# The delta-rule chain of a hybrid layer: full-height residual, cleared coupling block, loads as buffers come free, and a replanned schedule

## Chip, cores and metric

The kernel runs on one core of a Trainium2 chip. The metric is the device time of one launch in microseconds (us); the time of the kernel before is the median of three runs.

## What is computed

One layer of a streaming encoder over 2048 positions of width 1024, all in fp32. The part around the change is the gated DeltaNet branch, 8 heads of width 128 in chunks of 64 positions:

```python
A = jnp.where(strict, jnp.einsum('bhnik,bhnjk->bhnij', k_beta, k) * L, 0.0)
T = lax.linalg.triangular_solve(A + eye, eye, left_side=True, lower=True, unit_diagonal=True)
u = jnp.einsum('bhnij,bhnjv->bhniv', T, v * beta[..., None])
w = jnp.einsum('bhnij,bhnjk->bhnik', T, k_beta * jnp.exp(decay)[..., None])
def step(state, inp):
    v_new = u_c - jnp.einsum('bhck,bhkv->bhcv', w_c, state)
    o_c = q_c @ state + qk_c @ v_new
    state = state * a_c + jnp.einsum('bhck,bhcv->bhkv', k_c, v_new)
```

Around it stand an RMSNorm and one combined input projection ahead, a gMLP branch (gelu, LayerNorm, a masked 128x128 spatial mixing, a SiLU gate) beside it, and an output projection, a gated per-layer embedding and a last RMSNorm behind it.

## The kernel before

**Work.** The positions are taken in two passes of 1024. In each pass the projection (tile `pj`) goes through the heads; a head has three units of weights (k and q; v and the gMLP's u; the two gates z). Every projection product is three matmuls of 512 columns on rounded high and low parts (`mm3`: `hi*hi`, `hi*lo`, `lo*hi`). Behind the heads of both passes come the output projection (`pso`), the gate (`pg`) and the embedding.

**The branch of one head** runs as a row of tasks, two blocks of 512 positions each (b = 0, 1), four units of 128 positions (two chunks) per block:
- `decay` makes the mask tile `L` (POOL cuts it, line 184).
- `front` (line 729) transposes k into PSUM tile `pk`, squares it, makes `pkq` (k against k and q), and from it `AT`, the system's matrix times its mask (DVE), whose block [64:128, 0:64] couples the second chunk to the first (ACT). The diagonal blocks go to DRAM (`atd`).
- `root` and `side` make 1/norm of k (`iv`, a power on POOL) and the scaled v (`vn`); `side` transposes q and v (`pq`, `pvt`).
- `inverse` (line 833) solves the 64x64 triangular systems of the head on POOL: 63 columns, a multiply (`xtmp`) and a subtraction (`xs`) for each. The systems come back from DRAM four columns at a time in 16 loads `ain` with four buffers, issued on SP's queue; the solution goes to DRAM (`td`) and from there into the diagonal blocks of `AT` (here called `M`).
- `join` (line 883) multiplies the inverse of one chunk by the coupling block (`pgt`) and puts the product into the upper right block of `M`.
- `chain` (line 896) is the recurrence, eight units in a row for each head, each of four links that wait for one another: a matmul into `pc`, then an evacuation on DVE or ACT, then the next matmul. S to r: `pc<-S,kq`, then DVE makes the lower half of r in a tile `r0` whose upper half is zero. r0 to r: `pc<-r0,AT`, then ACT writes the lower half of `r` from PSUM and DVE its upper half. r to w: `pc<-r,AT`, then ACT writes the lower half of `w`, DVE the upper. w to S: `pc<-w,kd`, then DVE makes the new state S.
- `finish` (line 974) normalises the output (`sso`, a power on POOL), transposes it (`po_t`) and multiplies by the gate (`zb`).

The tiles `pk`, `pq`, `pvt`, `pgt` and `po_t` share two PSUM banks (tag "tr"), so each of their users waits until the one before last has been read.

**What sets the order.** The order of the instructions on every engine is planned by hand, in Python. `Flow` keeps a planned clock `fl.t` for PE, advanced by each matmul (lines 121 to 130), and one for DVE, ACT and POOL, advanced by a cost for each operation (lines 135 to 185). A task yields the planned time at which it wants to go on; until then the projection's matmuls are issued. So a chain link's planned duration says how many `pj` matmuls stand on PE between two matmuls of the chain. A delay `LAZY` says how long after its inputs a power or a mask is put on POOL. The costs set the order only; at run time every engine goes in its order and waits for semaphores.

Of the kernel before, what the change touches and what calls it, by code (L numbers as in the profile page):

```python
# [101 lines left out]

LAZY = 4000.0
CAPS = {"pj": 2, "tr": 2, "m": 2, "kq": 5, "pre": 2, "acc": 3, "uz": 3, "ot": 2, "gn": 2, "R": 2, "raw": 4, "w": 5}
# [3 lines left out]
def trunk(tc, a, out):  # L108
# [9 lines left out]
    def width(ap):  # L118
        return int(np.prod(ap.shape[1:]))
# [59 lines left out]
    def gtt(o, x, y, op, after=None):  # L179
        nc.gpsimd.tensor_tensor(o, x, y, op)  # L180
        return fl.op("pool", 375 + 1.95 * width(o), after)

# [4 lines left out]
    with ExitStack() as outer:  # L187
# [541 lines left out]
        def front(p, h, b, st):  # L729
# [9 lines left out]
            iv = gt("iv", "iv", [P, 4], 4)  # L739
            fb = gt("fb", "fb", [P, 4], 4)  # L740
            qe = gt("qe", "qe", [P, 4], 6)
            kd = gt("kd", "kd", [P, 4, P], 4)
# [13 lines left out]
            tt(bn, bn, beta[:, cs], ALU.mult)  # L756
            tt(fb, bn, ex[:, 3, cs], ALU.mult)
            fl.spawn(root(b, st, iv), f + LAZY - fl.t, 1)
            AT = gt("AT", "AT", [P, 4, P], 4)
            QK = gt("QK", "QK", [P, 4, P], 4)  # L760
            for u2 in range(2):
                while len(st["C"][b]) < 2:
                    yield fl.t + 300
                yield from fl.take("R", 2)
                hi = gt("R", "kqhi", [P, 2, 2, P], 2, F32R)
                lo = gt("R", "kqlo", [P, 2, 2, P], 2, F32R)
                yield from split_to(hi, lo, kq[:, u2 * 2:u2 * 2 + 2])
                yield fl.clk["dve"] + 120
                yield from fl.take("m")
                pkq = bank("m", "pkq", [P, 2, 2, P])  # L770
                for j in range(2):
                    for x, y in ((hi, hi), (hi, lo), (lo, hi)):
                        f = mm(pkq[:, j], x[:, j, 0], y[:, j], x is y, x is lo)
                fl.give("R")
                fl.give("R")
                while len(Ls) <= st["i"] + b:
                    yield fl.t + 300
                L = Ls[st["i"] + b]
                yield f
                for j in range(2):  # L780
                    u = u2 * 2 + j
                    yield from fl.room("dve")
                    f = stt(AT[:, u], pkq[:, j, 0], bn[:, u:u + 1], L[:, u], ALU.mult, ALU.mult)
                    act(AT[64:128, u, 0:64], pkq[64:128, j, 0, 0:64], AF.Copy, after=f,
                        scale=ex[64:128, 3, h * 8 + b * 4 + u:h * 8 + b * 4 + u + 1])
                yield from fl.room("dve")
                f = tt(QK[:, u2 * 2:u2 * 2 + 2], pkq[:, :, 1], L[:, u2 * 2:u2 * 2 + 2], ALU.mult)
                fl.give("m")
# [9 lines left out]
            fl.spawn(side(b, st, kq, vn, iv, ss, qe), 0, 2)  # L798
            st["B"].append((kq, kd, vn, AT, QK, bn, fb, qe))
            if b == 1:  # L800
# [32 lines left out]
        def inverse(p, h, st):  # L833
# [3 lines left out]
            def load(jc):  # L837
                ains[jc] = gt("ain", "ain", [P, 4, 64], 4)
                dma(ains[jc].rearrange("p j i -> p (j i)"),
                    asys[None, :, jc * 256:(jc + 1) * 256].to_broadcast([8, 16, 256]))  # L840
            while 2 * len(solved) < st["i"]:
                yield fl.t + 300
            xs = gt("xs", "xs", [P, 8, 64], 2)
            dma(xs, a["xinit"])
            load(0)
            while 2 * len(inverted) < st["i"]:
                yield fl.t + 300
            for jc in range(1, 4):
                load(jc)
            tmp = gt("xtmp", "xtmp", [P, 160], 1)  # L850
            yield fl.t + (1000 if h else 4500)
            for j in range(63):
# [8 lines left out]
                if jj == 3:  # L861
                    yield f
                    if jc < 12:
                        load(jc + 4)
                    elif jc == 12:
                        solved.append(1)
            yield f
            td = dp.tile([64, 2, 4, 2, 64], F32, tag="td", bufs=2, name="td")
            dma(td.rearrange("(k c) b u d i -> (c b u d) k i", c=8), xs)
            inverted.append(1)  # L870
            yield fl.t + 2600
# [11 lines left out]
        def join(b, st):  # L883
# [8 lines left out]
            fl.give("tr")  # L892
            yield f
            st["G"].append(b)

        def chain(p, h, st):
# [6 lines left out]
            for b in range(2):  # L903
                kq, kd, vn, M, QK, bn, fb, qe = st["B"][b]
                yield from fl.take("ot")
                ot = gt("ot", "ot", [P, 4, P], 2)
                sso = gt("sso", "sso", [P, 4], 2)
                for u in range(4):
# [7 lines left out]
                    if first:  # L916
                        f = vcopy(r0[lo], vn[lo, u])
                    else:
                        yield mm(pc[:, 0], kq[:, u, 0, :], Sp, True, True)
                        f = stt(r0[lo], pc[lo, 0], ne[lo, cu], vn[lo, u], ALU.mult, ALU.add)  # L920
                    yield f
                    f = mm(pc[:, 1], M[:, u], r0, True, True)
                    while outs[-1:] == [0]:
                        yield fl.t + 100
                    po = bank("o", "po", [P, 2, P])
                    if not first:
                        mm(po[:, 0], kq[:, u, 1, :], Sp, True, True)
                    yield f
                    f = act(r[lo], pc[lo, 1], AF.Copy, scale=-1.0)
                    if first:  # L930
                        f2 = vcopy(r[up], vn[up, u])
                    else:
                        f2 = stt(r[up], pc[up, 0], ne[up, cu], vn[up, u], ALU.mult, ALU.add)
                    yield max(f, f2)
                    while len(st["G"]) <= b:
                        yield fl.t + 100
                    f = mm(pc[:, 2], M[:, u], r, True, True)
                    yield f
                    f = act(w[lo], pc[lo, 1], AF.Copy, scale=bn[lo, uu])
                    yield max(f, ts(w[up], pc[up, 2], bn[up, uu], None, ALU.mult))  # L940
                    more = not (last and p == NPASS - 1)
# [5 lines left out]
                    if more:  # L947
                        yield f
                        Sn = gt("S", "S", [P, P], 2)
                        if first:  # L950
                            f = vcopy(Sn, pc[:, 3])
                        else:
                            f = stt(Sn, Sp, ex[:, 2, cu], pc[:, 3], ALU.mult, ALU.add)
                        Sp = Sn
                        yield f
                        if last:
                            dma(ssc[h], Sn)
# [364 lines left out]

        done, chained, fronts, solved, inverted, SC, mixed, stored, vdone, prepped, Ls = [[] for _ in range(11)]
        xready = [0, 0]
# [27 lines left out]
        X0 = x_tiles()  # L1352
        r0 = gt("r0", "r0", [P, P], 1)

        def setup():
            nc.vector.memset(r0, 0.0)
            fl.op("dve", 200)
            act(nega, nega, AF.Exp)
            ts(nega, nega, -1.0, None, ALU.mult)
            yield  # L1360
# [72 lines left out]
```

## Time and profile before

| | us |
|---|---|
| median of three runs | 2354.44 (2354.35 to 2355.75) |
| profiled execution, its own time | 2356.51 |
| its span | 2354.8 |
| PE matmul busy | 2284.6 (97%) |
| PE weight loads busy | 1873.9 (80%) |
| DVE busy | 1353.5 (57%) |
| ACT busy | 1115.8 (47%) |
| POOL busy | 1127.1 (48%) |
| mean granted TensorE clock | 0.993 |
| DMA moved | 254.59 MB, 108 GB/s |

The span is the profiler's, from first to last instruction; the execution's own time is what the device reported for the same run, so 1.7 us lie around the span. Busy times of PE overlap (a matmul's record begins before the one ahead has ended), so a PE that is 97% busy is not 3% from its floor. A bracket behind a row of the timeline is the idle time of the engine just before it and what ended it. Waits of an engine that nobody waits for cost nothing.

### The profile page before, as it was taken

How to read it: one execution, taken by the hardware profiler on the slowest of the kernel's cores; microseconds unless marked ns; L12 is line 12 of the kernel's file. 1: busy time of each engine (PE TensorE's matmuls, PEld its weight loads, DVE VectorE, ACT ScalarE, POOL GpSimd, SP SyncE). 2: the span in 40 equal slices, each digit the busy share in tenths (PEclk: the TensorE clock that was granted, in tenths of full speed). 3: DMA queues.
4: the chain of work that ended last, by engine and by line, in shares of the span. 5: the costliest groups of instructions: out<-in, count | busy, mean ns of one | idle time of the engine just before them, and what ended most of it. 6: DMA issues, size and time to landing. Idle time of an engine off the chain costs nothing.

```text
span 2354.8 us, 35453 instructions
## 1 busy us (share of the span) xinstructions
PE 2284.6 (97%) x11888; PEld 1873.9 (80%) x11888; DVE 1353.5 (57%) x2948; ACT 1115.8 (47%) x2665; POOL 1127.1 (48%) x2246
## 2 busy tenths in 40 slices
PE   8999999999999989999999999999999999999998
PEld 8978777777777779978787787777777878878886
DVE  5465566575675664456567567576564343246665
ACT  5554465464554643446446455464443232234443
POOL 1118677676676672147677667677680000001111
PEclk9999999999999999999999999999999999999999
DMA  5633332323323343223232332322453466452221
GB/s 188 222 105 97 99 87 75 96 68 100 97 78 98 90 131 100 82 77 89 81 96 70 98 100 70 106 76 81 124 177 109 144 202 195 139 186 65 81 81 63
DMA packets 269431, 254.59 MB, mean 108 GB/s; under 512 B 67904, under 2 KB 200512, under 8 KB 269248
## 3 DMA queue, kind: packets, MB, share of 16 engines
q1 hardware_dynamic: 269248, 252.32, 35.1%
q8 instruction: 93, 1.52, 0.3%
q14 instruction: 90, 0.74, 0.1%
HBM read 196.68 MB, written 55.57 MB: 107 GB/s over the span
## 4 chain that ended last, share of the span: by engine, by line
PE 76%; DVE 10%; ACT 7%; DMA 3%; issue 3%; SPq 1%; POOL 0%; ACTq 0%; DVEq 0%; POOLq 0%
PE pj L122 32%; PE pso L122 13%; PE pv L122 7%; PE pg L122 7%; PE pc L122 6%; DVE acc L153 2%; PE pe L122 2%; ACT junk L136 2%; PE po L122 2%; PE pm L122 1%; PE pgt L122 1%; PE pkq L122 1%; DVE wlo L149 1%; DVE AT L153 1%; ACT AT L136 1%
## 5 line engine op out<-in xcount | busy, mean ns | idle before, releaser
L180 POOL TENSOR_TENSOR xtmp<-ain,xs 128x132 f32<-128x132 f32 (+47 forms) x1008 | 464.6, 461 | 235.4 <-DMA ain<-atd 166.9
L180 POOL TENSOR_TENSOR xs<-xs,xtmp 128x132 f32<-128x132 f32 (+47 forms) x1008 | 480.1, 476 | 79.0
L176 POOL TENSOR_TENSOR rstd<-rstd,nhalf 128x1 f32<-128x1 f32 x64 | 46.0, 724 | 578.6 <-DVE rstd L160 297.6
L122 PE MATMUL pj<-xrhi,wlo 128*128 128x512 f32 x768 | 313.8, 409 | 0.0
L122 PE MATMUL pj<-xrhi,whi 128*128 128x512 f32 x768 | 309.3, 403 | 4.0 <-ACT u L136 4.0
L122 PE MATMUL pj<-xhi,wlo 128*128 128x512 f32 x768 | 310.2, 404 | 0.0
L122 PE MATMUL pj<-xhi,whi 128*128 128x512 f32 x768 | 310.1, 404 | 0.0
L122 PE MATMUL pj<-xlo,whi 128*128 128x512 f32 x768 | 310.0, 404 | 0.0
L122 PE MATMUL pj<-xrlo,whi 128*128 128x512 f32 x768 | 309.5, 403 | 0.0
L153 DVE SCALAR_TENSOR_TENSOR acc<-pre,cw,acc 128x512 f32<-128x512 f32 x288 | 226.9, 788 | 30.5 <-ACT acc L136 26.5
L149 DVE TENSOR_TENSOR wlo<-raw,whi 128x512 fp32r<-128x512 f32 x224 | 166.1, 746 | 83.4 <-ACT whi L136 82.1
L122 PE MATMUL pso<-wolo,yhi 128*128 128x512 f32 x512 | 204.7, 400 | 1.1 <-DVE wolo L149 1.1
L122 PE MATMUL pso<-wohi,ylo 128*128 128x512 f32 x512 | 204.8, 400 | 0.0
L122 PE MATMUL pso<-wohi,yhi 128*128 128x512 f32 x512 | 202.5, 395 | 1.2 <-ACT zb L136 1.2
L136 ACT ACTIVATE yhi<-yraw 128x512 fp32r<-128x512 f32 x128 | 80.2, 629 | 214.1 <-PE pso L122 202.4
L149 DVE TENSOR_TENSOR ylo<-yraw,yhi 128x512 fp32r<-128x512 f32 x128 | 89.5, 701 | 148.8 <-ACT yhi L136 146.5
L122 PEld LDWEIGHTS pj<-xrhi,whi 128*128 128x128 f32 x768 | 145.7, 190 | 30.0 <-ACT u L136 4.4
L122 PEld LDWEIGHTS pj<-xrlo,whi 128*128 128x128 f32 x768 | 145.3, 189 | 27.5
L122 PEld LDWEIGHTS pj<-xhi,wlo 128*128 128x128 f32 x768 | 145.1, 189 | 26.2
L122 PEld LDWEIGHTS pj<-xlo,whi 128*128 128x128 f32 x768 | 145.1, 189 | 25.7
L122 PEld LDWEIGHTS pj<-xhi,whi 128*128 128x128 f32 x768 | 145.2, 189 | 25.5
L122 PEld LDWEIGHTS pj<-xrhi,wlo 128*128 128x128 f32 x768 | 145.6, 190 | 25.0
(195 smaller groups left out, 4972.5 us busy)
## 6 DMA issues: line engine op xcount, KB each, us to landing
raw<-in_wu SPq DMA_DIRECT2D x224, 256.0 KB
ain<-atd SPq DMA_DIRECT2D x256, 128.0 KB
yraw<-ysc SPq DMA_DIRECT2D x128, 256.0 KB
vsc<-gv SPq DMA_DIRECT2D x64, 128.0 KB
gn<-vsc SPq DMA_DIRECT2D x32, 256.0 KB
ysc<-gn SPq DMA_DIRECT2D x32, 256.0 KB
ysc<-zb SPq DMA_DIRECT2D x32, 256.0 KB
wo<-in_wo SPq DMA_DIRECT2D x32, 256.0 KB
```

The costliest lines, as they stand in the source:

```text
L122: nc.tensor.matmul(o, lhsT, rhs, start=start, stop=stop)
L136: nc.scalar.activation(o, i, func, **kw)
L149: nc.vector.tensor_tensor(o, x, y, op)
L153: nc.vector.scalar_tensor_tensor(o, x, sc, y, op0, op1)
L176: nc.gpsimd.tensor_tensor(o, x, y, ALU.pow)
L180: nc.gpsimd.tensor_tensor(o, x, y, op)
```

## The change

1. Chain: `r` is made by one DVE operation over all 128 rows. The coupling block of `M` is cleared behind `join`, so that the first product needs no zero half; `r0` is gone. ACT then overwrites the lower half of `r`, and the lower half of `w` is made on ACT from `r` in SBUF with a new factor `nb` = -`bn`, no longer from PSUM beside DVE's half.
2. Planner: each link's planned end gets `SPARE` (120 ns) more; the links' ACT and DVE halves are no longer planned as parallel; the planned cost of POOL's solve operations goes down; `LAZY` from 4000 to 7000 ns.
3. `front`: the coupling blocks of two units are made by one DVE operation in place of two on ACT.
4. `inverse`: each of the first four loads of a system is issued as soon as one buffer is free in the plan, all behind the solution's `td` of the head before.

```diff
-LAZY = 4000.0
+LAZY = 7000.0
+SPARE = 120.0
...
     def gtt(o, x, y, op, after=None):
-        return fl.op("pool", 375 + 1.95 * width(o), after)
+        return fl.op("pool", 345 + 1.7 * width(o), after)
...
+            ts(nb, bn, -1.0, None, ALU.mult)
...
-                    f = stt(AT[:, u], pkq[:, j, 0], bn[:, u:u + 1], L[:, u], ALU.mult, ALU.mult)
-                    act(AT[64:128, u, 0:64], pkq[64:128, j, 0, 0:64], AF.Copy, after=f,
-                        scale=ex[64:128, 3, h * 8 + b * 4 + u:h * 8 + b * 4 + u + 1])
+                    stt(AT[:, u], pkq[:, j, 0], bn[:, u:u + 1], L[:, u], ALU.mult, ALU.mult)
+                us = slice(u2 * 2, u2 * 2 + 2)
+                c = h * 8 + b * 4 + u2 * 2
+                tt(AT[64:128, us, 0:64], pkq[64:128, :, 0, 0:64],
+                   ex[64:128, 3, c:c + 2, None].to_broadcast([64, 2, 64]), ALU.mult)
...
-            while 2 * len(solved) < st["i"]:
-                yield fl.t + 300
             xs = gt("xs", "xs", [P, 8, 64], 2)
-            dma(xs, a["xinit"])
-            load(0)
-            while 2 * len(inverted) < st["i"]:
-                yield fl.t + 300
-            for jc in range(1, 4):
+            for jc in range(4):
+                while len(solved) <= 2 * st["i"] - 4 + jc:
+                    yield fl.t + 300
+                if jc == 0:
+                    dma(xs, a["xinit"])
                 load(jc)
+                since = fl.t if jc == 0 else since
             tmp = gt("xtmp", "xtmp", [P, 160], 1)
-            yield fl.t + (1000 if h else 4500)
+            yield max(fl.t, since + 4500)
...
-                    elif jc == 12:
+                    else:
                         solved.append(1)
             yield f
+            solved.append(1)
...
-            yield f
+            nc.vector.memset(M[64:128, :, 0:64], 0.0)
+            yield fl.op("dve", 250) + SPARE
...
-                        f = stt(r0[lo], pc[lo, 0], ne[lo, cu], vn[lo, u], ALU.mult, ALU.add)
-                    yield f
-                    f = mm(pc[:, 1], M[:, u], r0, True, True)
+                        f = stt(r, pc[:, 0], ne[:, cu], vn[:, u], ALU.mult, ALU.add)
+                    yield f + SPARE
+                    while len(st["G"]) <= b:
+                        yield fl.t + 100
+                    f = mm(pc[:, 1], M[:, u], r, True, True)
...
-                    yield f
-                    f = act(r[lo], pc[lo, 1], AF.Copy, scale=-1.0)
-                    if first:
-                        f2 = vcopy(r[up], vn[up, u])
-                    else:
-                        f2 = stt(r[up], pc[up, 0], ne[up, cu], vn[up, u], ALU.mult, ALU.add)
-                    yield max(f, f2)
-                    while len(st["G"]) <= b:
-                        yield fl.t + 100
+                    yield f + SPARE
+                    yield act(r[lo], pc[lo, 1], AF.Copy, scale=-1.0) + SPARE
                     f = mm(pc[:, 2], M[:, u], r, True, True)
-                    yield f
-                    f = act(w[lo], pc[lo, 1], AF.Copy, scale=bn[lo, uu])
-                    yield max(f, ts(w[up], pc[up, 2], bn[up, uu], None, ALU.mult))
+                    act(w[lo], r[lo], AF.Copy, scale=nb[lo, uu])
+                    yield f + SPARE
+                    yield ts(w[up], pc[up, 2], bn[up, uu], None, ALU.mult) + SPARE
```

The order changes with the plan. **PE, the third unit of the fourth head's chain in the first pass**, before (`r_220` is the tile `r0`, `r` the full one):

```order
L122 MATMUL pc<-r_220,AT 128x128
L122 MATMUL po<-S,kq 128x128
L122 MATMUL pj<-xlo,whi 128x512
L122 MATMUL pj<-xhi,wlo 128x512
L122 MATMUL pc<-r,AT 128x128
L122 MATMUL pj<-xhi,whi 128x512
L122 MATMUL pj<-xlo,whi 128x512
L122 MATMUL pj<-xhi,wlo 128x512
L122 MATMUL pc<-w,kd 128x128
```

and the same unit now:

```order
L123 MATMUL pc<-r,AT 128x128
L123 MATMUL po<-S,kq 128x128
L123 MATMUL pj<-xhi,wlo 128x512
L123 MATMUL pj<-xhi,whi 128x512
L123 MATMUL pj<-xlo,whi 128x512
L123 MATMUL pc<-r,AT 128x128
L123 MATMUL pj<-xhi,wlo 128x512
L123 MATMUL pj<-xhi,whi 128x512
L123 MATMUL pj<-xlo,whi 128x512
L123 MATMUL pj<-xhi,wlo 128x512
L123 MATMUL pj<-xhi,whi 128x512
L123 MATMUL pc<-w,kd 128x128
```

Between the first and the second product with `AT` three projection matmuls stand where two stood, and ahead of the product with `w` five where three stood.

**SP's queue where the fourth head's solve ends**, before:

```order
L839 DMA ain<-atd 128x1x256 x2
L796 DMA atd<-AT 64x4x64 x2
L844 DMA xs<-in_xinit 128x512
L839 DMA ain<-atd 128x1x256
L650 DMA ws<-in_ws 128x128
L653 DMA bs<-in_bs 128x128
L253 DMA raw<-in_wu 128x512 x4
L660 DMA gn<-vsc_73 128x4x128 x2
L869 DMA td<-xs 128x8x64
L839 DMA ain<-atd 128x1x256 x3
L875 DMA AT<-td 64x4x64 x4
```

and now:

```order
L874 DMA td<-xs 128x8x64
L801 DMA atd<-AT 64x4x64 x2
L879 DMA AT<-td 64x4x64 x4
L851 DMA xs<-in_xinit 128x512
L844 DMA ain<-atd 128x1x256 x4
L651 DMA ws<-in_ws 128x128
L654 DMA bs<-in_bs 128x128
L254 DMA raw<-in_wu 128x512 x4
L661 DMA gn<-vsc_73 128x4x128 x2
```

The next head's `xs` and first `ain` stood ahead of `td`, and three further `ain` between `td` and `AT<-td`; now `td`, the second half of `atd` and `AT<-td` stand ahead of all of them, and the loads of weights behind.

**PE, the transposes of the sixth head's front** (k in `pk`, q in `pq`) beside those of a finished output block (`po_t`), before:

```order
L122 MATMUL pj<-xhi,whi 128x512
L128 MATMUL po_t<-ident,ot 128x128 x4
L128 MATMUL pk<-ident,kq 128x128 x4
L122 MATMUL pj<-xlo,whi 128x512
L128 MATMUL pq<-ident,kq 128x128 x4
L122 MATMUL pj<-xhi,wlo 128x512
```

and now:

```order
L129 MATMUL pq<-ident,kq 128x128 x4
L129 MATMUL pk<-ident,kq 128x128 x4
L123 MATMUL pj<-xhi,wlo 128x512
L123 MATMUL pj<-xhi,whi 128x512
L123 MATMUL pj<-xlo,whi 128x512
L123 MATMUL pj<-xhi,wlo 128x512
L123 MATMUL pj<-xhi,whi 128x512
L123 MATMUL pj<-xlo,whi 128x512
L123 MATMUL pj<-xhi,wlo 128x512
L123 MATMUL pj<-xhi,whi 128x512
L123 MATMUL pj<-xlo,whi 128x512
L129 MATMUL po_t<-ident,ot 128x128 x4
```

`po_t` no longer stands directly ahead of the front's transposes but nine projection matmuls behind them.

## Rows read from the trace of the kernel before

**Rows 1.** PE by line: instructions | busy us, mean ns | idle before, releasers.

```profile
L122 PE MATMUL pc<-r,AT 128*128 128x128 f32 x512 | 109.0, 295 | 6.9 <-DVE r L153 0.9
L122 PE MATMUL pc<-w,kd 128*128 128x128 f32 x240 | 54.6, 309 | 7.2 <-DVE w L158 2.6
L122 PE MATMUL pc<-S,kq 128*128 128x128 f32 x240 | 51.7, 297 | 3.9 <-DVE S L153 2.9 <-DMA S<-ssc 0.7
```

**Rows 2.** Tile pc: waits of its weight loads on PE, us and times.

```profile
  PEld pc L122: 104.4, 277
```

**Rows 3.** Timeline, the third unit of the fourth head's chain: start, duration, engine.

```profile
558.05 0.39 PE L122 MATMUL pc<-r,AT 128*128 128x128 f32 x2
...
558.54 0.27 ACT L136 ACTIVATE r<-pc 64x128 f32<-64x128 f32 x1 [1.52 <-PE pc L122]
...
558.74 0.39 PE L122 MATMUL pj<-xhi,wlo 128*128 128x512 f32 x1
558.84 0.36 DVE L153 SCALAR_TENSOR_TENSOR r<-pc,ne,vn 64x128 f32<-64x128 f32 x1 [1.82 <-ACT r L136]
...
559.25 0.49 PE L122 MATMUL pc<-r,AT 128*128 128x128 f32 x2
...
559.50 0.48 PE L122 MATMUL pj<-xhi,whi 128*128 128x512 f32 x1
...
559.78 0.36 ACT L136 ACTIVATE w<-pc,bn 64x128 f32<-64x128 f32 x1 [0.97 <-PE pc L122]
559.82 0.40 PE L122 MATMUL pj<-xlo,whi 128*128 128x512 f32 x1
...
560.05 0.39 PE L122 MATMUL pj<-xhi,wlo 128*128 128x512 f32 x1
560.18 0.36 DVE L158 TENSOR_SCALAR w<-pc,bn 64x128 f32<-64x128 f32 x1 [0.20 <-ACT w L136]
...
560.59 0.49 PE L122 MATMUL pc<-w,kd 128*128 128x128 f32 x2
```

**Rows 4.** Timeline, weight loads: the first and the last late link.

```profile
269.48 0.30 PEld L122 LDWEIGHTS pc<-w,kd 128*128 128x128 f32 x2 [0.33 <-DVE w L158]
...
1820.59 0.30 PEld L122 LDWEIGHTS pc<-r,AT 128*128 128x128 f32 x2 [0.56 <-DVE r L153]
```

**Rows 5.** Timeline, POOL through one solve and to the start of the next.

```profile
533.16 0.29 POOL L180 TENSOR_TENSOR xtmp<-ain,xs 128x63 f32<-128x63 f32 x1 [3.06 <-DMA ain<-atd]
...
542.51 0.29 POOL L180 TENSOR_TENSOR xtmp<-ain,xs 128x59 f32<-128x59 f32 x1 [5.77 <-DMA ain<-atd]
...
569.10 1.01 POOL L176 TENSOR_TENSOR sso<-sso,nhalf 128x4 f32<-128x4 f32 x1 [3.79 <-DVE sso L153]
...
591.22 0.89 POOL L184 TENSOR_SCALAR_AFFINE_SELECT L<-L 128x512 f32<-128x512 f32 x1 [2.74 <-ACT L L136]
...
622.25 0.66 POOL L180 TENSOR_TENSOR xs<-xs,xtmp 128x8 f32<-128x8 f32 x1
...
627.75 0.56 POOL L180 TENSOR_TENSOR xtmp<-ain,xs 128x63 f32<-128x63 f32 x1 [4.85 <-DMA ain<-atd]
```

**Rows 6.** Timeline, SP's queue as that solve begins: issue time, issue duration.

```profile
529.46 0.63 SPq L839 DMA_DIRECT2D ain<-atd  x1
...
536.95 0.45 SPq L869 DMA_DIRECT2D td<-xs  x1
...
541.39 2.58 SPq L875 DMA_DIRECT2D AT<-td  x4
```

**Rows 7.** PE by line, the transposes of k.

```profile
L128 PE MATMUL pk<-ident,kq 128*128 128x128 f32 x128 | 19.6, 276 | 6.1 <-DVE zb L153 5.6 <-ACT kq L136 0.5
```

**Rows 8.** Timeline, PE, the last head of the first pass.

```profile
832.62 0.92 PE L122 MATMUL pgt<-AT 128*128 128x64 f32 x6 [3.96 <-DMA AT<-td]
```

**Rows 9.** Windows: stretch, length, busy of PE, PEld, DVE, ACT, POOL, granted clock, DMA.

```profile
833.00:840.00 7.00, 6.95 (x27) 5.69 (x26) 1.96 (x5) 1.11 (x3) 5.83 (x16) 0.52 0.26 66
```

**Rows 10.** ACT by line, the coupling blocks.

```profile
L136 ACT ACTIVATE AT<-pkq,ex 64x64 f32<-64x64 f32 x128 | 39.5, 309 | 109.3 <-DVE AT L153 107.9 <-DMA raw<-in_wu 1.2
```

More of the change, by code (lines that the diff above doesn't have):

```diff
@@ L740, in front @@
             fb = gt("fb", "fb", [P, 4], 4)
+            nb = gt("nb", "nb", [P, 4], 4)
             qe = gt("qe", "qe", [P, 4], 6)
@@ L798, in front @@
             fl.spawn(side(b, st, kq, vn, iv, ss, qe), 0, 2)
-            st["B"].append((kq, kd, vn, AT, QK, bn, fb, qe))
+            st["B"].append((kq, kd, vn, AT, QK, bn, fb, qe, nb))
             if b == 1:
@@ L864, in inverse @@
                         load(jc + 4)
-                    elif jc == 12:
+                    else:
                         solved.append(1)
             yield f
+            solved.append(1)
             td = dp.tile([64, 2, 4, 2, 64], F32, tag="td", bufs=2, name="td")
             dma(td.rearrange("(k c) b u d i -> (c b u d) k i", c=8), xs)
-            inverted.append(1)
             yield fl.t + 2600
@@ L903, in chain @@
             for b in range(2):
-                kq, kd, vn, M, QK, bn, fb, qe = st["B"][b]
+                kq, kd, vn, M, QK, bn, fb, qe, nb = st["B"][b]
                 yield from fl.take("ot")
@@ L916, in chain @@
                     if first:
-                        f = vcopy(r0[lo], vn[lo, u])
+                        f = vcopy(r, vn[:, u])
                     else:
-                        yield mm(pc[:, 0], kq[:, u, 0, :], Sp, True, True)
-                        f = stt(r0[lo], pc[lo, 0], ne[lo, cu], vn[lo, u], ALU.mult, ALU.add)
-                    yield f
-                    f = mm(pc[:, 1], M[:, u], r0, True, True)
+                        yield mm(pc[:, 0], kq[:, u, 0, :], Sp, True, True) + SPARE
+                        f = stt(r, pc[:, 0], ne[:, cu], vn[:, u], ALU.mult, ALU.add)
[3 more added lines that the diff above has]
+                    f = mm(pc[:, 1], M[:, u], r, True, True)
                     while outs[-1:] == [0]:
@@ L947, in chain @@
                     if more:
-                        yield f
+                        yield f + SPARE
                         Sn = gt("S", "S", [P, P], 2)
@@ L954, in chain @@
                         Sp = Sn
-                        yield f
+                        yield f + SPARE
                         if last:
@@ L1321, in stream @@
             yield from out_stream()
-        done, chained, fronts, solved, inverted, SC, mixed, stored, vdone, prepped, Ls = [[] for _ in range(11)]
+        done, chained, fronts, solved, SC, mixed, stored, vdone, prepped, Ls = [[] for _ in range(10)]
         xready = [0, 0]
@@ L1352, in trunk @@
         X0 = x_tiles()
-        r0 = gt("r0", "r0", [P, P], 1)
         def setup():
-            nc.vector.memset(r0, 0.0)
-            fl.op("dve", 200)
             act(nega, nega, AF.Exp)
```

## Prediction

> **What bounds the kernel now.** PE's matmul rows are busy for 2284.6 of 2354.8 us and no other engine for more than 57% (table above), and the change keeps PE's 10840 matmuls as they are: the order lists the same number before and after. So only time that PE stands waiting can go, and only where PE waits does the change matter.
>
> I looked first at the lines of PE, for the idle time of the chain's matmuls. They show 6.9 + 7.2 + 3.9 = 18.0 us [rows 1]. The view of who waited for tile `pc` shows 104.4 us in 277 waits of its weight loads [rows 2]. The two differ by a factor of six, so I went to the timeline, one unit of one head [rows 3]. Two projection matmuls with nothing between them start 0.23 us apart (559.82 and 560.05). The second product with `AT` starts 0.51 us after the projection matmul ahead of it (558.74 to 559.25), so it is 0.51 - 0.23 = 0.28 us late, and the product with `w` 0.54 - 0.23 = 0.31 us late (560.05 to 560.59). Behind each, one projection matmul comes late again: 559.50 to 559.82 is 0.32, another 0.09. None of this is "idle" of a matmul row, because the record of the matmul ahead still covers it; and the weight load's wait is longer than the loss, 0.56 for the last late link [rows 4], since it begins while the array still works. What counts is the spacing of the starts.
>
> Done so for all 481 links of the chain between 269.48 and 1820.59 [rows 4], 218 are late and lose 63.4 us, some 0.29 each: r0 to r 86 links and 24.5 us, r to w 78 and 24.9, w to S 50 and 12.5, S to r 4 and 1.5. That is the stock from which this change can draw.
>
> **The change part by part.**
>
> *Links with one hop less.* In [rows 3] ACT's half of `r` ends at 558.81 and DVE's half at 559.20: DVE stands behind ACT, since both write one tile, and PE waits for both, 1.20 us from product to product. Without DVE's half the link is 0.39 shorter, 0.81. For `w` ACT ends at 560.14 and DVE at 560.54: 0.40 less, 0.94 in place of 1.34. By the order, what stands between grows too: three projection matmuls with the `po` product for two at the first link (+0.23), five for three at the second (+0.46). So in this unit the first link has 0.39 + 0.23 - 0.28 = 0.34 to spare, the second 0.40 + 0.46 - 0.31 = 0.55. For w to S, where nothing is shortened, only the larger planned distance helps; its mean loss of 0.25 is about one projection matmul, and the order gives it at least that at nearly every unit. I count the whole 63.4 as gone, less what remains because DVE or ACT is busy with other work when a link comes due. For that no row gives a price; it lies between 0 and half, 32, and I take 10, since the spare of 0.34 and 0.55 is more than the usual loss of 0.29 and only an operation in the way that is longer than the spare still costs something. Result: -63.4 + 10 = -53.4.
>
> *Full height of r, clearing, factor, coupling.* DVE loses the 120 upper halves of `r`. A full-height operation on the same 128 columns I take at the same 0.36 [rows 3]; at worst twice that, no dearer than the two halves. It gains 64 coupling operations, 32 clears and 32 small factors, at most 0.36 each by the same rows, [rows 3]: 46 us against 120 x 0.36 = 43 given up. ACT loses 128 x 0.309 = 39.5 us, and with them a place where it stood 109.3 us waiting for DVE [rows 10]. None of this lies on the path: DVE is idle for 43% of the span, ACT for 53%. I set it at 0. The clear is the one with a waiter: the head's first product with `M` now stands behind `join` and the clear. Planned projection matmuls cover it; without the cover it costs 0.36 at 16 heads, 5.8. Four more loads of ACT's function table (the order counts 119 for 115) go into the 10.
>
> *Transposes.* `pk` waited 6.1 us for a tr bank that DVE had to read for `zb` [rows 7]. By the order `po_t` moves from directly ahead of the front's transposes to nine projection matmuls behind them. But `po_t` now waits behind `pk` in its turn. Half goes: -3, between -6.1 and 0.
>
> *Solve, loads and later powers.* One solve takes 622.25 + 0.66 - 533.16 = 89.75 us, and in it POOL stands for 5.77 (a load `ain`), 3.79 (`sso`) and 2.74 (`L`) [rows 5]. Loads ahead and the later powers and masks are to take these away: 89.75 - 12.30 = 77.45. In return the next solve starts later. Its loads stand behind `td` and `AT<-td` now, so from a solve's end: `td` to `AT<-td` 541.39 - 536.95 = 4.44, the four issues 2.58, the issues of `xs` and the first `ain` at 0.63 each 1.3, from `ain`'s issue to the first column 533.16 - 529.46 = 3.70 [rows 5, 6]: 12.0 in all, 13.3 where two `atd` issues (0.65 each, a quarter of the 2.58) come between. The loop takes 89.4 to 90.8 us per head. PE's head period is now 627.75 - 533.16 = 94.6 [rows 5], and 56.4 saved over 16 heads make it 91.1. So the loop just fits. Because the margin is 0.3 to 1.7 us, I count one further wait of `pgt` for `AT<-td` like the one there is: 3.96 idle [rows 8], then 7.00 us at a granted clock of 0.52, the 1.2 GHz level [rows 9], which costs 7.00 x 0.48 = 3.4. Together +7.4; the ends are -7.4 (the present one goes as well) and the rival on the loop below.
>
> Sum: -53.4 - 3 + 7.4 = -49.0. The profiled execution took 2356.51, so 2307.5; the median of the runs is 2.1 below that execution, so **2305**.
>
> **The rivals.**
>
> *Half the lateness stays*, because links wait for engines and not for the plan: DVE and ACT do other work between. For it: S to r and w to S have no hop to lose. Against it: ACT and DVE are both idle for about half of the time. -31.7 - 3 + 7.4 = -27.3, 2327. Chance 0.17.
>
> *The loop of solve and loads becomes the bound* (the case on the other side). Its place is POOL at the start of each solve and PE at `pgt`. Half of the 12.30 us of waits in the solve stay, say: 83.6 + 12.7 = 96.3 against 91.1, so PE waits 5.2 us at each of 14 steps from head to head, and falls to 1.2 GHz behind each, 3.4 us more by [rows 8, 9]. 14 x 8.6 = 120 in place of the 7.4: -56.4 + 120 = +64, 2418. It decides from 56.4 / 14 = 4.0 us a head, that is from where the wait exceeds 0.6 us with the clock's loss or 4.0 without it: a loop of 91.7 to 95.1. For it: the margin above is under 2 us, and POOL's queue keeps powers and masks in its middle. Against it: `td` no longer stands behind four loads of weights. The Trainium skill ("TensorE: Matmul & The Clock Gate", section "HAM oscillation — how this bites in real kernels") says that a matmul loop which waits for a DMA in every turn is throttled anew in every turn; the one wait there agrees, and no row here shows a repeated one. Chance 0.22, of it 0.15 slower, 0.01 same and 0.06 with waits so short that it stays between forecast and break-even, about 2330.
>
> *Weight loads are the true measure.* If PE lost all that its weight loads waited, 104.4 [rows 2], the gain were -104.4 + 10 - 3 + 7.4 = -90, 2264. The timeline [rows 3, 4] speaks against it: a late link shows a wait of 0.56 and starts 0.28 late. The Trainium skill ("Perfetto Trace Analysis", section "Identifying the Most-Contended Engine") holds the busy time of matmuls a bad measure, as they are pipelined, and that of weight loads a good one; the trace agrees with the first half, 18.0 against 63.4, and lies between the two views. Chance 0.04.
>
> *The links don't get shorter in time.* PE's lateness only moves: the same projection matmuls are spent earlier, and other tasks lack them later. At best the 18.0 of [rows 1] goes, -18 - 3 + 7.4 = -13.6, 2341; at worst nothing, 2352 to 2354. Chance 0.07, of it 0.03 faster, 0.04 same.
>
> **How the numbers follow.** Forecast 0.50, with its own range 2278 (all 63.4, all 6.1 and the wait of [rows 8] go: -76.9) to 2326 (20 of lateness, nothing at `pk`, two waits: -28.6). With half the lateness 0.17, short waits 0.06 and the last rival 0.07 it makes 0.80, so the range is 2278 to 2352; the weight loads' case below and the loop's above stay out, 0.20. A run of this kernel can tell some 0.2%, 4.7 us, from no change: faster 0.50 + 0.17 + 0.06 + 0.04 + 0.03 = 0.80, same 0.05, slower 0.15.
>
> **What would show it.** Right: weight-load waits of `pc` fall from 104.4 to below 30, the product with `r` starts on the spacing of the projection, ACT's `w` starts before PE's second product has ended, POOL shows no wait for `ain` inside a solve, and the head period is 91 us. Wrong: a wait of `pgt` for `AT<-td` in most heads with a lower granted clock behind it (the loop); `pc` waits for DVE as before behind operations like `gn` or `acc` (half stays); fewer `pc` waits but longer ones at `pkq`, `pk` or `po_t` (it only moves).

## Result and profile after

The changed kernel takes 2273.72 us, median of 4 runs (2270.92 to 2275.31), against 2354.39 for the kernel before: ratio 0.9656, 95% interval [0.9639, 0.9673], 81 us faster. The forecast was 49 us less, 2305, with a range from 2278 to 2352; the time lies 4 us below the range.

The profiled execution took 2273.43 us, its span 2271.7. The engines, from the page:

```profile
PE 2228.3 (98%) x11888; PEld 1888.4 (83%) x11888; DVE 1335.0 (59%) x2947; ACT 1078.3 (47%) x2541; POOL 1120.3 (49%) x2246
```

The lines of PE that answer to [rows 1] and [rows 7], with those of `pkq`, `pgt`, `po_t` and `pq`, and the wait of `pc`'s weight loads that answers to [rows 2]:

```profile
L123 PE MATMUL pc<-r,AT 128*128 128x128 f32 x512 | 99.5, 276 | 7.9 <-ACT r L137 6.8 <-DVE r L154 0.9
L123 PE MATMUL pc<-w,kd 128*128 128x128 f32 x240 | 47.3, 278 | 2.8 <-DVE w L159 1.8 <-ACT w L137 0.9
L123 PE MATMUL pc<-S,kq 128*128 128x128 f32 x240 | 47.0, 277 | 0.1
L123 PE MATMUL pkq<-kqlo,kqhi 128*128 128x256 f32 x128 | 37.7, 294 | 2.9 <-DVE kqlo L150 2.8
L123 PE MATMUL pgt<-AT 128*128 128x64 f32 x256 | 31.5, 270 | 0.5 <-DVE AT L150 0.5
L129 PE MATMUL po_t<-ident,ot 128*128 128x128 f32 x128 | 19.5, 275 | 7.8 <-DVE kd L150 7.2 <-DVE ot L150 0.4 <-DVE iv L159 0.2
L129 PE MATMUL pk<-ident,kq 128*128 128x128 f32 x128 | 19.2, 272 | 0.0
L129 PE MATMUL pq<-ident,kq 128*128 128x128 f32 x128 | 19.2, 272 | 0.0
...
  PEld pc L123: 12.8, 14
```

`pk` no longer waits, `pgt` no longer waits for `AT<-td`, and the weight loads of `pc` wait 12.8 us where they waited 104.4. More idle time than before show only `po_t` (4.0 us before, 7.8 now) and the products with `AT` (6.9 and 7.9, of it 6.44 one wait in the last head).

The same unit as in [rows 3], the third of the fourth head's chain, in the timeline of the changed kernel:

```profile
534.89 0.35 DVE L154 SCALAR_TENSOR_TENSOR r<-pc,ne,vn 128x128 f32<-128x128 f32 x1 [0.23 <-PE pc L123]
...
535.84 0.39 PE L123 MATMUL pc<-r,AT 128*128 128x128 f32 x2
...
536.33 0.27 ACT L137 ACTIVATE r<-pc 64x128 f32<-64x128 f32 x1 [1.23 <-PE pc L123]
536.52 0.39 PE L123 MATMUL pj<-xhi,whi 128*128 128x512 f32 x1
536.63 0.40 ACT L137 ACTIVATE w<-r,nb 64x128 f32<-64x128 f32 x1
536.75 0.39 PE L123 MATMUL pj<-xlo,whi 128*128 128x512 f32 x1
536.98 0.38 PE L123 MATMUL pc<-r,AT 128*128 128x128 f32 x2
...
537.40 0.36 DVE L159 TENSOR_SCALAR w<-pc,bn 64x128 f32<-64x128 f32 x1 [2.16 <-PE pc L123]
```

ACT's half of `r` ends at 536.60, 0.38 before the product that needs it, and that product starts on the projection's spacing, 0.23 behind the matmul ahead. ACT's half of `w` is done before DVE's half begins.

**Where the 83 us of the two profiled executions lie.** As in the prediction, what counts is the spacing of starts. I took every pair of neighbouring matmul rows of PE, subtracted the spacing that the first has when nothing is late (0.23 us at 512 columns, 0.12 at 256, 0.11 at 128) and summed what is over 0.04, by the tile of the second row. All kernels of this study, us, "tr" for `pk`, `pq`, `pvt` and `po_t` together:

```
                        own time   sum late    pc    pkq    tr   pgt   rest
before                   2356.5     196.0    65.3   13.1   21.4   5.5  90.7
changed                  2273.4     113.9    17.7    7.2   10.0   1.0  78.0
e1 old ops, new distance 2315.0     155.0    61.2    8.3    4.5   1.1  79.9
e2 no SPARE              2280.3     118.6    30.6    9.9    0.5   0.2  77.4
e3 all but chain         2341.1     180.5    90.0    8.4    0.5   1.3  80.3
e4 chain only            2308.1     148.4    19.7   22.5   15.3  11.8  79.1
e5 old loads             2293.0     133.1    28.5   14.7    1.5   2.9  85.5
e6 LAZY 4000             2297.5     138.9    39.3    9.0    3.7   3.8  83.1
e7 coupling on ACT       2290.6     131.2    17.8   20.9   11.6   1.8  79.1
e8 old POOL costs        2282.2     123.1    18.4    8.1    5.6   6.5  84.5
e9 chain and coupling    2278.0     118.7    20.6   10.0    5.7   4.5  77.9
e10 later feed           2263.4     104.1    11.0    6.7    9.9   1.0  75.5
e11 later feed, po_t     2261.4     102.7    13.4    7.0    5.5   0.0  76.8
e12 later feed, 180      2285.6     125.4    29.0    5.9   10.8   1.0  78.7
e13 coupling only        2329.8     169.0    62.0    7.0    7.8   6.6  85.6
e14 coupling on ACT last 2282.4     123.0    23.4    9.5    1.9   2.0  86.2
```

A kernel's own time less its sum is 2158.6 to 2161.7 in all sixteen. So the sum of late starts is the whole difference between these kernels, to 3 us in 95, although their PE shows as 97 to 99% busy. All sixteen have the same matmuls, so this had to come out nearly so: the table says where the time goes, and the experiments have to say why. Some 48 to 51 us of the rest, in every kernel, is no lateness: a projection matmul right behind a pair of 128-column halves is followed at 0.32 in place of 0.23, late pair or not. The rest also holds most of what PE loses at the 1.2 GHz level.

### The profile page after: what moved, and what is told of

The parts are those of the page before. It is cut to its first block, busy times and chain, and to the rows that moved or that the text cites. A ratio compares the mean times of both kernels' runs of the same rounds, so it can differ in the third digit from the quotient of the medians.

```text
span 2271.7 us, 35525 instructions
## 1 busy us (share of the span) xinstructions
PE 2228.3 (98%) x11888; PEld 1888.4 (83%) x11888; DVE 1335.0 (59%) x2947; ACT 1078.3 (47%) x2541; POOL 1120.3 (49%) x2246
## 4 chain that ended last, share of the span: by engine, by line
PE 87%; DVE 3%; ACT 3%; DMA 3%; POOL 1%; issue 1%; SPq 1%; DVEq 0%; POOLq 0%; ACTq 0%
PE pj L123 41%; PE pso L123 15%; PE pg L123 8%; PE pv L123 7%; PE pc L123 5%; PE po L123 2%; PE pkq L123 2%; PE pe L123 2%; ACT junk L137 1%; PE pm L123 1%; PE pgt L123 1%; PE po_t L129 1%; DMA ws<-in_ws 1%; PE ph L129 1%; PE pq L129 1%
## 5 line engine op out<-in xcount | busy, mean ns | idle before, releaser
L137 ACT ACTIVATE whi<-raw 128x512 fp32r<-128x512 f32 x224 | 139.1, 625 | 62.4 <-PE pj L123 25.8
```

The costliest lines, as they stand in the source:

```text
L137: nc.scalar.activation(o, i, func, **kw)
```

## The experiments

Each kernel ran beside the kernel before on the same chip; "+" and "-" in the diffs are against the changed kernel where nothing else is said.

**The chain: hop or distance?** Old operations with the new planned distances:

```diff
-                        f = stt(r, pc[:, 0], ne[:, cu], vn[:, u], ALU.mult, ALU.add)
+                        f = stt(r0[lo], pc[lo, 0], ne[lo, cu], vn[lo, u], ALU.mult, ALU.add)
...
-                    yield act(r[lo], pc[lo, 1], AF.Copy, scale=-1.0) + SPARE
+                    f = act(r[lo], pc[lo, 1], AF.Copy, scale=-1.0) + SPARE
...
+                        f2 = stt(r[up], pc[up, 0], ne[up, cu], vn[up, u], ALU.mult, ALU.add)
+                    yield f
...
-                    act(w[lo], r[lo], AF.Copy, scale=nb[lo, uu])
+                    act(w[lo], pc[lo, 1], AF.Copy, scale=bn[lo, uu])
```

> The changed kernel with the chain's operations of before (r0 and half-height r on DVE behind ACT, w from PSUM on both engines, no clearing), but with the changed kernel's planned distances between the links. Theory A (the hop saved and the larger distance each carry a part): a link from r0 to r takes 1.20 us and gets 1.03 from product to product at 82 places, r to w 1.34 and gets 1.28 at 58: some 30 us of the chain's lateness stay, against 17 in the changed kernel; time 2285 to 2295. Theory B (the distance alone does it): within 5 us of the changed kernel's 2273.7. Theory C (the hop alone does it): lateness back near 63 us, 2315 to 2325.

Measured 2315.72, ratio 0.9844 [0.9827, 0.9862]: 42 us slower than the changed kernel. The chain's lateness is 61.2, three and a half times that of the changed kernel; sum and time are theory C's (the hop alone), but the links do not bear it out. r0 to r loses 22.3 at 75 links and r to w 12.8 at 27, together 35 where theory A's figures give 17 (82 x 0.17 and 58 x 0.06), and S to r, which I had left at nothing, loses 22.1 at 15 links. Of this last, 8.7 is one wait behind the load of `yraw` (see the faster version below), and four of 1.7 to 2.9 stand behind DVE, which waits there for the load of `ws`. What the distances bring with the old operations shows beside "all but the chain" below, which has the old distances too and all else as here: it takes 2339.96, 24 us more, and the two links lose 76 there for 35.

New operations without the distance:

```diff
-SPARE = 120.0
+SPARE = 0.0
```

> The changed kernel with SPARE at 0: new operations, distances between links nearly as in the kernel before (medians 0.69 us of other matmuls from r to r, 0.70 from r to w, 0.69 from w to S). Theory A: r to r is on time (0.81 needed, 0.80 given), r to w is 0.14 late, w to S as late as before (12.5 us): lateness of the chain 25 to 35 us, 2285 to 2295. Theory B (distance alone): lateness near 63, 2315 to 2325. Theory C (hop alone): within 5 us of 2273.7.

2282.44, ratio 0.9696 [0.9682, 0.9711]: 9 us slower, just below theory A's bounds. The chain's lateness is 30.6. So of the chain's gain the shorter links carry the larger part, 42 us with the new distances and 58 without them; the distances bring 9 us behind the shorter links and 24 without them.

**The parts one by one.** Chain and join as before, all else changed; and the kernel before with the changed chain and join alone:

> The changed kernel with chain and join wholly as before (operations and distances); loads as buffers come free, later powers, the coupling on DVE and POOL's planned costs stay. If the chain's lateness and the other parts add up: the chain's 46 to 53 us come back, 2320 to 2327. If the other gains (transposes, pgt, clock) hang on the chain's order: up to the time of before, 2354. If the other parts alone already bring most: below 2300.

> The kernel before with the changed chain and join alone (operations and SPARE distances); loads, LAZY, coupling on ACT and POOL's planned costs as before. If the parts add up: 2354.4 less 46 to 53, that is 2301 to 2308. If a shorter head period without the faster solve runs into the solve (89.8 us with its waits, restart 4.9 us): waits of pgt for AT<-td, a lower clock behind them, and 2320 or more. If the chain brings everything: 2275.

All but the chain: 2339.96, ratio 0.994 [0.9925, 0.9955]. The chain alone: 2310.27, ratio 0.9814 [0.9794, 0.9835], 44 us. Taking the chain out costs 66, putting it in brings 44: the parts do not add up. In the chain alone `pc` is late by 19.7 only, but `pkq` by 22.5 for 13.1 and `pgt` by 11.8 for 5.5: of 45.6 gained in the chain 15.7 are given back there, while the tr banks and the rest bring 17.7. The lines of that kernel that show it, on PE, and what ACT and DVE waited for:

```profile
L123 PE MATMUL pkq<-kqlo,kqhi 128*128 128x256 f32 x128 | 40.3, 315 | 12.2 <-DVE kqlo L150 12.1
L123 PE MATMUL pgt<-AT 128*128 128x64 f32 x256 | 33.2, 280 | 9.3 <-DMA AT<-td 9.2
...
ACT AT L137 <- DVE AT L154: 110.6, 112, 3.2
DVE AT L154 <- ACT AT L137: 26.3, 62, 1.3
DVE QK L150 <- ACT AT L137: 21.5, 57, 0.4
```

**The schedule's parts, undone one at a time.** Loads as before; LAZY back at 4000; coupling on ACT; POOL's old planned costs:

> The changed kernel with the system's loads issued as before: xs and the first load when the head before is nearly solved, three more only behind td, each solve planned from there. Theory A (the loads are what lets the shorter head period stand): POOL's waits for ain inside the solve come back, some 6 us a head, and td stands behind weight loads in SP's queue; pgt waits for AT<-td in most heads, time 2295 to 2330. Theory B (the later powers and masks alone keep the solve short): the solve stays below 78 us, time within 5 us of 2273.7.

> The changed kernel with LAZY at 4000 again. Theory A (later powers keep the solve short): POOL waits again for sso, iv and L, 4 to 7 us a solve, the loop of solve and restart grows from 89.6 to some 95 us against a head period of 90: PE waits 4 to 5 us at pgt in most heads, 2335 or more, above 2380 if the granted clock falls each time. Theory B (the inputs were long there): solve 75 to 77 us, time within 5 us of 2273.7.

> The changed kernel with the coupling blocks on ACT again, two operations for one on DVE, each behind DVE's AT. Theory A (ACT standing behind DVE there held up what PE waits for): waits for DVE's AT of some 100 us on ACT return and pkq's lateness rises from 7 towards 13 or more; time 2280 to 2290. Theory B (ACT has the room): within 5 us of 2273.7.

> The changed kernel with POOL's solve operations planned at the old, higher cost: the solve is planned some 6 us longer than it takes. Theory A (a loop planned at its true length gives the short head period): the planner puts each pgt later, more projection matmuls between heads and fewer among the links; head period the same or longer, the chain's lateness up, 2280 to 2300. Theory B (the planned cost does not decide): within 5 us of 2273.7.

2289.10, 2298.67, 2292.75 and 2285.91; ratios 0.972 [0.9706, 0.9735], 0.9771 [0.9745, 0.9798], 0.9739 [0.9722, 0.9756], 0.9704 [0.9689, 0.9718]. Old loads: the time fell between the theories and not in theory A's way, since the solves stay at 70 to 78 us and `pgt` never waits for `AT<-td`; of the 19 us of lateness more, 7.5 are `pkq`; the longest wait, 9.5 at 1635.5, stands behind the load of `yraw`, for which the changed kernel has a wait of 6.6 too. LAZY 4000: solves of 74 to 82 us, and four heads of the first pass wait 2.1 to 3.2 us for the clear behind `pgt`, less than theory A's 4 to 5 in most heads and not by its way: ahead of the clear DVE stands 5.5 to 6.8 us for the load of `ws`. POOL's old costs: solves of 76 to 86 us and 5 us of `pgt` waiting for `AT<-td`, theory A's size by another way. Coupling on ACT: theory A, 3 us above its bounds, `pkq` at 20.9 for 7.2.

Undone singly, the chain and these four cost 66 + 15 + 25 + 19 + 12 = 137 us, far more than the 81 there are. Any change of a planned cost re-plans everything behind it, and taking a part out of a tuned plan costs something in itself. One such cost shows in the traces: DVE clears a block of the weights tile `ws` behind its load, and the plan has no such wait. In the kernel before DVE stands 2.6 us for it in all, in the changed one 33.7, with LAZY at 4000 66.1; one head of that kernel:

```profile
523.40 0.11 DVE L652 MEMSET ws<- 64x64 f32 x1 [5.56 <-DMA ws<-in_ws]
...
524.17 0.27 DVE L897 MEMSET AT<- 64x256 f32 x1
...
524.49 0.49 PE L123 MATMUL pc<-r,AT 128*128 128x128 f32 x2 [2.08 <-DVE AT L897]
```

Parts put in, from before, tell more:

**Chain and coupling together**, the rest as before (against the chain alone):

```diff
-                    act(AT[64:128, u, 0:64], pkq[64:128, j, 0, 0:64], AF.Copy, after=f,
-                        scale=ex[64:128, 3, h * 8 + b * 4 + u:h * 8 + b * 4 + u + 1])
...
+                tt(AT[64:128, us, 0:64], pkq[64:128, :, 0, 0:64],
+                   ex[64:128, 3, c:c + 2, None].to_broadcast([64, 2, 64]), ALU.mult)
```

> The chain alone (the earlier run at 2310.3) with the coupling blocks on DVE as well; loads, LAZY and POOL's planned costs as in the kernel before. Theory A (the coupling on ACT held up kqhi, which stands behind it on ACT, and so pkq, in any schedule): pkq's lateness falls from 22.5 to 10 or less; time 2292 to 2300, and what the schedule then gives is the rest to 2273.7. Theory B (the coupling only mattered under the new schedule): 2305 to 2312, pkq above 18.

2278.46, ratio 0.968 [0.9665, 0.9694]: 32 us from that one edit, better than theory A expected, and only 5 us from the changed kernel, with intervals that overlap. Here the loads, LAZY and planned costs are the old ones, and so is the solve. Its first and last operation on POOL, for the fifth head:

```profile
515.87 0.29 POOL L181 TENSOR_TENSOR xtmp<-ain,xs 128x63 f32<-128x63 f32 x1
...
605.24 0.21 POOL L181 TENSOR_TENSOR xs<-xs,xtmp 128x8 f32<-128x8 f32 x1
```

89.6 us, as in [rows 5], and the start of the next follows 3.4 later. This is the longest step; from head to head it takes 86 to 93 us, 89 on the mean, and `pgt` waits 3.4 us in the whole run. In the changed kernel the solve takes 75.6, and POOL then stands 14 us for the loads:

```profile
521.68 0.64 POOL L181 TENSOR_TENSOR xtmp<-ain,xs 128x63 f32<-128x63 f32 x1 [14.05 <-DMA ain<-atd]
...
596.73 0.59 POOL L181 TENSOR_TENSOR xs<-xs,xtmp 128x8 f32<-128x8 f32 x1
...
612.36 0.29 POOL L181 TENSOR_TENSOR xtmp<-ain,xs 128x63 f32<-128x63 f32 x1 [14.07 <-DMA ain<-atd]
```

Both loops fit in a head period of 90 us on the mean. So the new loads, LAZY and planned costs bring at most some 5 us beside chain and coupling. Without the chain they bring nothing: all but the chain takes 2339.96, 10 us more than the coupling alone, which follows.

**The coupling alone, and how it works.** The kernel before with the coupling on DVE and nothing else; and the chain alone with the coupling still on ACT, but behind DVE's `QK` (the edit of this one, against the chain alone):

```diff
-                    f = stt(AT[:, u], pkq[:, j, 0], bn[:, u:u + 1], L[:, u], ALU.mult, ALU.mult)
-                    act(AT[64:128, u, 0:64], pkq[64:128, j, 0, 0:64], AF.Copy, after=f,
-                        scale=ex[64:128, 3, h * 8 + b * 4 + u:h * 8 + b * 4 + u + 1])
-                yield from fl.room("dve")
+                    stt(AT[:, u], pkq[:, j, 0], bn[:, u:u + 1], L[:, u], ALU.mult, ALU.mult)
+                yield from fl.room("dve")
                 f = tt(QK[:, u2 * 2:u2 * 2 + 2], pkq[:, :, 1], L[:, u2 * 2:u2 * 2 + 2], ALU.mult)
+                for j in range(2):
+                    u = u2 * 2 + j
+                    act(AT[64:128, u, 0:64], pkq[64:128, j, 0, 0:64], AF.Copy, after=f, ...)
```

> The kernel before with the coupling blocks on DVE and nothing else changed. Theory A (the coupling is worth the same in any surrounding: with the chain it gave 2310.3 to 2278.5, 32 us): 2318 to 2326. Theory B (it pays only once the chain is no longer late, because before PE lost the time in the chain anyway): 2338 to 2354.

> The chain alone (2310.3), with the coupling still on ACT, but both its operations behind DVE's QK, so that DVE waits for ACT nowhere there; ACT still waits for DVE, and kqhi still stands behind on ACT. Theory A1 (ACT's queue holds kqhi): pkq's lateness stays above 18, time 2304 to 2315. Theory A2 (DVE, stopped twice to three times a block behind ACT's halves, comes late to kqlo, kd and zb): pkq's lateness falls to 10 or less, 2278 to 2292.

The coupling alone: 2330.15, ratio 0.9901 [0.9886, 0.9916], 23 us; between the theories. The chain alone brings 44 and both 76, so some 9 us belong to both together. The coupling on ACT but last: 2282.97, ratio 0.9703 [0.9685, 0.9721], 27 us better than the chain alone and theory A2. ACT still stands 68.8 us for DVE (110.6 in the chain alone), but DVE waits for ACT nowhere there, and `pkq` is late by 9.5 in place of 22.5:

```profile
ACT AT L137 <- DVE QK L150: 68.8, 53, 3.0
...
L123 PE MATMUL pkq<-kqlo,kqhi 128*128 128x256 f32 x128 | 38.1, 297 | 3.9 <-DVE kqlo L150 3.8
```

ACT keeps its 39.5 us of work and most of its standing, and still 27 of the 32 us come back. So the larger part of the cost was DVE's stops. One block of the front in the changed kernel with the coupling on ACT shows them:

```profile
601.82 0.34 DVE L154 SCALAR_TENSOR_TENSOR AT<-pkq,bn,L 128x128 f32<-128x128 f32 x1
602.19 0.31 ACT L137 ACTIVATE AT<-pkq,ex 64x64 f32<-64x64 f32 x1 [2.69 <-DVE AT L154]
602.53 0.35 DVE L154 SCALAR_TENSOR_TENSOR AT<-pkq,bn,L 128x128 f32<-128x128 f32 x1 [0.38 <-ACT AT L137]
602.92 0.31 ACT L137 ACTIVATE AT<-pkq,ex 64x64 f32<-64x64 f32 x1 [0.42 <-DVE AT L154]
603.26 0.63 ACT L137 ACTIVATE kqhi<-kq 128x512 fp32r<-128x512 f32 x1
603.26 0.42 DVE L150 TENSOR_TENSOR QK<-pkq,L 128x256 f32<-128x256 f32 x1 [0.38 <-ACT AT L137]
603.92 0.69 DVE L150 TENSOR_TENSOR kqlo<-kq,kqhi 128x512 fp32r<-128x512 f32 x1 [0.23 <-ACT kqhi L137]
```

DVE stops twice for 0.38 behind an ACT operation, and so in nearly all of the 64 blocks (124 stops). The plan has no such stop, since it gives `QK` and the second `AT` no operation of ACT to wait for. `QK` needs nothing that ACT makes; it reads the same PSUM tile. The Trainium skill ("PSUM — Partial Sum Buffer", section "PSUM bank collisions raise a hardware error") says that the scheduler of the compiler's back end sets a dependency between any two instructions on different engines that touch the same bank and quadrant of partitions, reads included; the trace agrees, with 57 such waits of `QK` and 21.5 us in the kernel with the chain alone; what set the order in these kernels it does not show. What stands behind on DVE comes later by that: by the table `pkq` (22.5 late with the stops, 9.5 without), the users of the tr banks (15.3 and 1.9) and `pgt` (11.8 and 2.0). The chain's own matmuls show none of it (19.7 and 23.4).

**A faster version.** In the changed kernel PE's longest wait of the chain is in the last head (PE, ACT and SP from the timeline):

```profile
1606.28 2.96 SPq L1023 DMA_DIRECT2D wo<-in_wo  x6
1609.29 2.81 SPq L1070 DMA_DIRECT2D yraw<-ysc  x4
...
1615.32 0.63 ACT L137 ACTIVATE yhi<-yraw 128x512 fp32r<-128x512 f32 x1 [9.69 <-DMA yraw<-ysc]
...
1616.64 0.80 PE L123 MATMUL pc<-r,AT 128*128 128x128 f32 x2 [6.44 <-ACT r L137]
```

ACT stands 9.7 us, up to 1615.3, for a load that was issued from 1609.3 on behind six others, and the chain's `r` stands behind it; the first matmul that uses `yhi` starts at 1648.6. PE then runs at the 1.2 GHz level until 1622 (granted clock 0.50 from 1616 to 1622), which by an estimate costs 0.5 x 5.6 = 2.8 us more. Three versions:

```diff
+                if i == 0:
+                    yield fl.t + 12000
                 yield from fl.take("w")
                 hi = wp.tile([P, 4, P], F32R, tag="whi", name="yhi")
```

> The changed kernel with the first split of the output projection's input (yhi) planned 12 us behind its load. Theory A (ACT stood 9.7 us waiting for yraw at 1606, and the last head's product with r behind it, 6.6 us late, then 1.2 GHz for some us): this wait goes, 2263 to 2268. Theory B (the loads crowd at that point and the next consumer waits as long): within 4 us of 2273.7.

> As the run before it in this list, and po_t planned 2 us later, away from kd, which holds its bank: if po_t's lateness of 9.4 us goes and nothing takes its place, 4 to 8 us faster than that run; if the place is taken by pk or pq, no faster.

> As the later feed alone, with SPARE at 180. Theory A (the chain's last lateness, some 10 us, is engines busy with other work, which distance covers): 3 to 8 us faster than the later feed alone. Theory B (larger distances lengthen the chain beyond the head period or crowd other tasks): slower than it by 5 or more.

The later feed: 2264.60, ratio 0.9618 [0.9604, 0.9632], as theory A has it, 9 us better than the changed kernel. With `po_t` 2 us later: 2261.86, ratio 0.9608 [0.9594, 0.9623], the fastest of the study; `tr` falls from 9.9 to 5.5, less than I expected, and its interval overlaps the run before it. SPARE at 180: 2286.09, ratio 0.971 [0.9694, 0.9727], 21 us worse, theory B: solves of 82 to 86 us in three heads of the second pass, whose chains then start 3.5 to 6.3 us late. At these three places too DVE stands for the load of `ws`, for 5.9 to 8.7 us.

## Why the prediction was right and wrong

By the table the two profiled executions differ by 47.6 us in the chain (forecast 53.4), 11.4 at the transposes (3), 4.5 at `pgt` (7.4 more instead of less, of it 3.4 for the clock), and by 5.9 at `pkq` and 12.7 in the rest, for which there was no term. With the coupling back on ACT the changed kernel takes 2292.75, 12 us from the forecast and inside its range.

- **Chain, -53.4: right in mechanism and size, for its own matmuls.** The late links lost 63.4; now they lose 17.2, of which 6.6 is the one wait for `yraw` that has nothing to do with the links. Without it 10.6 remain, where I had put 10; no row gave that a price, so the closeness is luck. What I did not see is that in the chain alone a third of this gain is taken back at `pkq` and `pgt`, behind DVE's stops. One reading was wrong without effect on the sum: the "0.09 late" of the projection matmul behind a late link is its usual spacing behind a pair of 128-column halves; the second loss of 0.10 is between the two halves of the late product itself.
- **"None of this lies on the path: DVE is idle for 43% of the span, ACT for 53%. I set it at 0": this step failed.** The coupling's move is worth 23 us alone and 32 beside the chain. I counted busy time and read the 109.3 us of idle in [rows 10] as ACT's own affair. I did not ask what DVE waits for there, nor what is queued behind on DVE. It is the same hop between two engines on one tile that I had costed in the chain, at another place. The view of waits of the kernel before shows it, 47 us in 121 waits (us in total, times, longest):

```profile
DVE AT L153 <- ACT AT L136: 24.2, 61, 1.0
DVE QK L149 <- ACT AT L136: 23.0, 60, 0.5
```

- **"Half goes: -3" for the transposes: too small.** `pk` and `pq` were 13.9 late before and 0.4 now. They are 1.2 with the coupling alone and 5.5 with chain and coupling, but 2.3 also in the changed kernel with the coupling on ACT, in which DVE still stops. So DVE's stops are not the whole of it, and how much is the move of `po_t`, as I had it, is not shown. `po_t` got 4.5 more. Together the four tiles fell from 21.4 to 10.0.
- **"I count one further wait of pgt": +7.4, wrong in sign.** The wait of [rows 8] went too. The terms of the loop were right: the solve fell to 75 us (77.45 forecast), the restart from a solve's end to the next start rose to 12.5 to 16.2 (12.0 to 13.3), the period is 90 (91.1). But the loop with the old loads fits as well, so the risk that took 0.22 of the chances was none that this part of the change brought or averted. That does not make it void: with the solve planned otherwise (LAZY 4000, POOL's old costs, SPARE 180) waits of 2 to 6 us came back, at `pgt` or at the chain's start, the latter behind DVE's wait for `ws`.
- **Range and chances.** The low end summed the three terms I had, each at its best, -76.9. The fourth, set at 0, had no end of its own; with the 19 us that the coupling is worth in the changed kernel the low end would have been 2259, and the range would have held the time. Of the rivals, that weight loads are the true measure (2264) came nearest to the time, but not by its reason: their waits fell by 91.6 us and the chain's lateness by 47.6.

## What to carry to other kernels

Where two engines write halves of one tile or read one PSUM tile in turn, each pays the other's operation and the hand-over, and what is queued behind them pays too: give both halves to one engine, or put the second engine's part behind the first engine's whole run, before thinking about which of them is busier. Measure a PE-bound kernel by the spacing of its matmul starts; the busy share, 97% before and 98% after, hid 83 us here. In a plan that orders all engines, judge a part by putting it into the old kernel, not only by taking it out of the new one, and look for waits that the plan does not know of: a read of a shared tile by another engine, a load that an engine stands for.

## What the runs showed of the hardware

A DVE operation over all 128 partitions took as long as over 64, at the same 128 columns; the line of the kernel before and of the changed one:

```profile
L153 DVE SCALAR_TENSOR_TENSOR r<-pc,ne,vn 64x128 f32<-64x128 f32 x240 | 83.5, 348 | 103.7 <-ACT r L136 86.2 <-PE pc L122 16.2
```

```profile
L154 DVE SCALAR_TENSOR_TENSOR r<-pc,ne,vn 128x128 f32<-128x128 f32 x120 | 41.6, 347 | 30.1 <-PE pc L123 27.9 <-ACT whi L137 0.9
```

The clock did not fall behind every wait of PE. In the kernel with LAZY at 4000, two heads wait for the clear for about the same time, PE idle for 2.1 us up to 524.5 and for 2.4 up to 615.7; the granted clock around them, from its windows (length, busy time of PE, PEld, DVE, ACT and POOL, clock, DMA share, GB/s):

```profile
614.00:624.00 10.00, 8.26 (x37) 7.06 (x38) 4.23 (x12) 4.16 (x9) 8.36 (x22) 0.83 0.53 173
520.00:530.00 10.00, 7.92 (x47) 6.62 (x47) 3.51 (x11) 2.57 (x6) 8.12 (x25) 1.00 0.70 212
```

Behind the one it fell to the 1.2 GHz level for a part of the window, which cost 10 x 0.17 = 1.7 us, half of what I had priced; behind the other it did not fall at all.
